# adaLN columns on the tensor engine in float32, four column groups at a time, in a two-layer hybrid diffusion trunk

## The chip, the cores and the metric

One core of a Trainium2 chip runs the whole program in one launch. The metric is the device time of that launch in microseconds (us). The engines are PE (the tensor engine; PEld is its weight load), DVE (vector), ACT (scalar), POOL (GpSimd) and SP, whose queue issues most of the DMAs. Every engine works through its own instructions in order, and waits on semaphores where it needs another's result.

## The reference, cut to what matters

Two layers work on 128 context tokens and 512 latent tokens of 1024 channels. Each layer takes six modulation vectors of 1024 channels (a shift, a scale and a gate for each of its two halves) from a conditioning vector, one set for the context tokens and one for the latent tokens:

```python
mod = silu(c) @ w_mod + b_mod        # c: c_ctx for the context tokens, c for the latent ones
sh1, sc1, g1, sh2, sc2, g2 = jnp.split(mod, 6, axis=-1)
h = rmsnorm(x, p['norm1_g']) * (1.0 + sc1) + sh1
y, s_fin = parallel_mixer(h, s0, p)  # DeltaNet, Hyena, FNet, gated merge
x = x + g1 * y
h = rmsnorm(x, p['norm2_g']) * (1.0 + sc2) + sh2
x = x + g2 * swiglu(h, p['w_gu'], p['w_down'])
```

All arrays are float32. `w_mod` has 2 x 1024 x 6144 elements, so each layer's modulation reads 24 MB for two vectors.

## The kernel before

Channels lie on the 128 partitions and tokens along them: a tensor of 1024 channels is eight tiles of 128 x 640. An "adaLN column" is 128 consecutive outputs of the modulation, so a layer has 48: 0 to 7 are the shift and 8 to 15 the scale of the first norm, 16 to 23 the first gate, 24 to 39 the shift and scale of the second norm, 40 to 47 the second gate. `self.mod[l]` holds them as [128, 2 vectors, 48].

The large products run in three fp32r products each (weights and activations are split into a high and a low part, `wh`/`wl` on the weight side), 320 tokens at a time (`gemm`, `mm3`). ACT writes a unit's high part and POOL its low part. Raw weight tiles `wr` come in two turning buffers through the SP queue (`wload`). The second sub-layer (`ffn`) computes each pair of a gate and an up tile with seven block products instead of eight (`pair`), and the sums that this takes, of weights (`wsum`) and of results (`add` in `pair`), are DVE's.

The order of instructions is fixed when the kernel is built. A main stream issues the large products; side streams (norms, filters, scans, adaLN) are generators whose steps are slipped in by `pump`, after every second contraction tile, as soon as a count of engine time kept by `tick` says that their inputs are there. A step yields a `hint`, a time by which the next one may be issued early. `finish` issues what is left of a stream.

adaLN is computed in two ways. `mods_pe` (line 720) makes columns 0 to 11 of layer 0: the stationary operand is 128 x 2 (the two conditioning vectors), the moving one 128 x 512 of `w_mod` (tiles `A<-in_wm`), in float32, and the rows that result are turned by small products against the identity. `mods` (line 675) makes all other columns on DVE, from a transposed `w_mod` and a copy of both vectors on every partition (`cs`, 1 MB, input `cc`): a column is two 128 x 512 loads into `U` buffers and four multiply-and-sum instructions, whose sums land in `mh`, and one small instruction adds halves and bias into `mod`. Each multiply-and-sum shows as two rows of the trace, `CUSTOM_DVE_ANT_0 A<-U,A` and `DVE_READ_ACCUMULATOR2_ANT mh<-`. `mods` runs five times:

- columns 12 to 27 of layer 0 from the start on, beside the first norm and the input projection (line 2122)
- 28 to 37 of layer 0, or 34 to 39 of layer 1, beside the gates of branch a (line 1887)
- 38 to 47 of layer 0, or 40 to 47 of layer 1, beside the merge of branch b and the output projection (line 1922), finished before the second norm
- 0 to 33 of layer 1 beside layer 0's second sub-layer (line 2139)

The first norm of layer 0 needs columns 0 to 15. `rstd` makes 1 / rms, and `norm` writes `na` (gain times 1 + scale) and then the tiles of h.

Of the kernel before, what the change touches and what calls it, by code (L numbers as in the profile page):

```python
# [18 lines left out]
P = 128  # L19
D = 1024  # L20
# [14 lines left out]
MP = 3  # L35
# [36 lines left out]
def _plan():  # L72
    """the order of use: whole tiles, and pairs of a gate and an up tile for the seven products"""
    p = [("w", k) for k in _stream() if k[0] not in ("g", "u", "d")]
    for kind, g in _ffn_order():
        if kind == "gu":
            for j in GROUPS[g]:
                p += [("s", j)] if j >= WHOLE else [("w", ("g", j)), ("w", ("u", j))]
        else:
            p += [("w", ("d", g, m)) for m in range(0, 8, 2)]  # L80
    return p
# [9 lines left out]
def _parked(key):  # L91
    """whether the split tile stays for one half of the tokens after the other, in a place of its own"""
    k, m = (key[0], key[-1]) if isinstance(key, tuple) else (None, None)
    return (k == "o" and m >= O_SPLIT or k in ("g", "u") and m == 1 or k == "in" and m // P in QKV_ORDER[1:Q_SPLIT]
            or k == "d" and key[1] == len(GROUPS) - 1 and m >= D_SPLIT)
# [10 lines left out]
# ---------------------------------------------------------------- tables that depend on shapes alone  # L106
# [126 lines left out]
# ---------------------------------------------------------------- layout of the inputs  # L233
# [5 lines left out]
def _pack(i):  # L239
# [4 lines left out]
    o["cc"] = np.broadcast_to(np.stack([f["c_ctx"], f["c"][0]])[None], (P, 2, D))  # L244
    o["cT"] = np.stack([f["c_ctx"], f["c"][0]]).reshape(2, KD, P).transpose(2, 1, 0)
    o["wm0"] = f["w_mod"][0][:, :512 * MP].reshape(2, 4, P, MP, 512).transpose(3, 0, 2, 1, 4).reshape(MP, 2, P, 2048)
    o["wmod"] = f["w_mod"].transpose(0, 2, 1).reshape(DEPTH, 48, P, D)
# [53 lines left out]
class _Net:  # L301
# [21 lines left out]
    # ---- allocation  # L323
# [19 lines left out]
    def xps(self):  # L343
        """a bank of either pool"""
        self.nps += 1
        return self.ps() if self.nps % 2 else self.gps()
# [8 lines left out]
    # ---- background work: each step of a side stream is issued once the tensor engine's work issued  # L355
    # so far reaches, by the engines' rates, the time when the step's inputs are there
    def when(self, *aps):
        """the time when what was issued has written these"""
# [8 lines left out]
    def tick(self, eng, op, out, ins):  # L367
# [9 lines left out]
        else:  # L377
            if eng == "pe":
                dt = max(n, 64) * (1 if ins[0].dtype != F32 else 4 if ins[0].shape[0] > 64 else 2) / 2.4e3 + 0.007
# [15 lines left out]
    def on(self, *tiles):  # L395
        """the next step of the stream that runs needs these"""
        self.cur.t = max(self.cur.t, self.when(*[x[:] if not hasattr(x, "ap") else x for x in tiles]))

    def at(self, *tiles):
        """the next step of the stream that runs needs these and nothing of its other steps"""  # L400
# [7 lines left out]
    def ready(self, co):  # L408
        """a stream may yield a test (the time when it is met, or None) or a time its next step may
        be issued early"""  # L410
# [18 lines left out]
    def pump(self):  # L429
        """the streams' ready steps, as long as the main stream keeps its share of the tensor engine"""  # L430
# [19 lines left out]
    def finish_one(self, cos):  # L450
        """the next step of several streams, or of one that they wait for"""
# [6 lines left out]
    def stagger(self, gens, width):  # L458
        """several streams, `width` at a time, each behind the one before it"""
# [32 lines left out]
    # ---- weights  # L492
    def wplan(self, depth):
        """raw tiles in the order of their loads, and units: up to 512 columns that are split at once"""
# [24 lines left out]
    def wload(self, need=-1):  # L519
        """loads of raw tiles up to `need`, and further ones whose room is free by now"""  # L520
# [10 lines left out]
    def wsum(self, r, x):  # L531
        """sums of the four blocks of a gate and an up tile"""
# [12 lines left out]
    def wsplit(self, n):  # L545
        """units up to n, split in two float32r parts"""
# [29 lines left out]
    def wget(self, key):  # L576
        """the units of the next item: all at once, or of a pair one after the other"""
# [13 lines left out]
    def lots(self, n):  # L591
        """places for the next n parked units"""
# [6 lines left out]
    def free(self, seen, drop):  # L599
        """so many more units have come to use, and so many of those in turning buffers had their last"""  # L600
# [32 lines left out]
    def rsqrt(self, r, m):  # L633
        """r = m ** -0.5, Newton's steps from a guess by the bits of m"""
# [9 lines left out]
    # ---- start  # L644
# [30 lines left out]
    def mods(self, l, lo, hi, par=False, ahead=1, hint=0.5):  # L675
        """adaLN columns lo..hi (of 48) of layer l, one per output channel tile"""
# [6 lines left out]
        S = self.A()  # L683
        cs = S[:, 0:2 * D].rearrange("p (s d) -> p s d", s=2)
        ju = S[:, 2 * D:AW]
        nc.sync.dma_start(cs, self.I["cc"])
        q = []

        def load():
            n = at[0]  # L690
            if n < 2 * (hi - lo):
                q.append(self.U())
                nc.sync.dma_start(q[-1], self.I["wmod"][l, lo + n // 2, :, 512 * (n % 2):512 * (n % 2) + 512])
                at[0] += 1

        at = [0]
        for _ in range(ahead):
            load()
        self.on(q[0], cs)
        yield  # L700
        nc.scalar.activation(cs, cs, AF.Silu)
        yield
        for n in range(2 * (hi - lo)):
            j, i = lo + n // 2, n % 2
            if i == 0:
                hv = self.p2.tile([P, 2, 2], F32, tag="mh", name=self.nm("mh"))
            r = q.pop(0)
            if len(q) < (ahead if n < 4 else 1):
                load()
            for s in range(2):  # L710
                nc.vector.tensor_tensor_reduce(out=ju, in0=r, in1=cs[:, s, 512 * i:512 * i + 512], op0=ALU.mult,
                                               op1=ALU.add, scale=1.0, scalar=0.0, accum_out=hv[:, i, s:s + 1])
            if i:
                nc.vector.scalar_tensor_tensor(out=mv[:, :, j], in0=hv[:, 0], scalar=self.par[l][0][:, C_BMOD + j:C_BMOD + j + 1],
                                               in1=hv[:, 1], op0=ALU.add, op1=ALU.add)
            if q:
                self.on(q[0])
            yield hint

    def mods_pe(self):  # L720
        """the first 4 * MP adaLN columns of layer 0, on the tensor engine"""
        nc = self.nc
        mv = self.mod[0] = self.p2.tile([P, 2, 48], F32, tag="mod", name=self.nm("mod"))
        ct = self.p2.tile([P, KD, 2], F32, tag="ct", name=self.nm("ct"), bufs=1)
        nc.sync.dma_start(ct, self.I["cT"])
        nc.scalar.activation(ct, ct, AF.Silu)
        w = {}

        def load(j):
            if j < 2 * MP:  # L730
                w[j] = self.A()
                nc.sync.dma_start(w[j][:, :2048], self.I["wm0"][j // 2, j % 2])

        for j in range(6):
            load(j)
            if j == 3:
                yield
        yield
        pt = self.ps()
        row = {}  # L740

        def turn(j):
            for k in range(4):
                n = 4 * j + k
                nc.tensor.transpose(pt[:, 2 * n:2 * n + 2], row[j][0:2, k * P:k * P + P], self.ident[0:2, 0:2])

        for j in range(MP):
            ps = self.ps()
            for i in range(2):
                self.on(w[2 * j + i])  # L750
                yield
                for k in range(4):
                    nc.tensor.matmul(ps[0:2, :512], ct[:, 4 * i + k], w[2 * j + i][:, k * 512:k * 512 + 512],
                                     start=i == 0 and k == 0, stop=i == 1 and k == 3)
                load(2 * j + i + 6)
                if j and not i:
                    turn(j - 1)
            row[j] = self.Tt()
            nc.scalar.copy(row[j][0:2, :512], ps[0:2])
        yield  # L760
        turn(MP - 1)
        n = 4 * MP
        for s in range(2):
            nc.vector.tensor_tensor(out=mv[:, s, 0:n], in0=pt[:, :2 * n].rearrange("p (j s) -> p s j", s=2)[:, s],
                                    in1=self.par[0][0][:, C_BMOD:C_BMOD + n], op=ALU.add)

    # ---- RMSNorm
    def sq_add(self, k, c=None):
        """running sum of the squares of x's channel tile k, on all tokens or a chunk of them"""
# [11 lines left out]
    def rstd(self, u, n, w):  # L781
        """1 / rms(x) of n * w tokens from u on, on all partitions"""
# [23 lines left out]
    def wait(self, c):  # L806
        """for 1 / rms(x) of a chunk"""
# [3 lines left out]
    def norm(self, l, gcol, sh, scl, new, place):  # L811
        """h = rmsnorm(x) * (1 + sc) + sh, split in two float32r parts"""
# [37 lines left out]
    def need(self, n):  # L850
        """steps of the norm until n channel tiles of chunks of h are issued"""
# [13 lines left out]
    def norm_blocks(self, l, gcol, sh, scl):  # L865
        """h by blocks (half of the channels) x (half of the tokens), and the sums of blocks for the seven
        products"""
# [34 lines left out]
    # ---- x in and out of DRAM  # L902
# [4 lines left out]
    # ---- Hyena's filters  # L907
    def sin_mlp(self, ps, M, scale, bias, out, n):
        """out = sin(scale * ps + bias), the argument brought within half a turn first"""
# [1326 lines left out]
```

## Time and profile before

| | |
|---|---|
| median of 3 runs | 2922.06 us (2921.55 to 2927.12) |
| span of the profiled execution | 2920.5 us |
| PE busy | 2570.7 us, 88% |
| DVE busy | 2191.0 us, 75% |
| POOL busy | 1372.3 us, 47% |
| ACT busy | 1017.4 us, 35% |
| HBM read | 294.89 MB |

PE is the busiest engine, but the share of the span is an average over stages; rows of stretches tell more. A float32 matmul shows as two records (two passes), an fp32r one as one. Every instruction stands under one line, because a helper records it, so rows are told apart by the names of their tiles: `pg` and `ps` are accumulators, `wh` and `wl` the split weights, `mh` and `mod` belong to adaLN.

### The profile page before, as it was taken

How to read it: one execution, taken by the hardware profiler on the slowest of the kernel's cores; microseconds unless marked ns; L12 is line 12 of the kernel's file. 1: busy time of each engine (PE TensorE's matmuls, PEld its weight loads, DVE VectorE, ACT ScalarE, POOL GpSimd, SP SyncE). 2: the span in 40 equal slices, each digit the busy share in tenths (PEclk: the TensorE clock that was granted, in tenths of full speed). 3: DMA queues.
4: the chain of work that ended last, by engine and by line, in shares of the span. 5: the costliest groups of instructions: out<-in, count | busy, mean ns of one | idle time of the engine just before them, and what ended most of it. 6: DMA issues, size and time to landing. Idle time of an engine off the chain costs nothing. (4 is left out here: it accounts for less than half of the span.)

```text
span 2920.5 us, 53508 instructions
## 1 busy us (share of the span) xinstructions
PE 2570.7 (88%) x20996; PEld 2423.8 (83%) x20996; DVE 2191.0 (75%) x4162; ACT 1017.4 (35%) x2148; POOL 1372.3 (47%) x1228
## 2 busy tenths in 40 slices
PE   5897879879998888888898988788899988999998
PEld 1686878879998888878897768788899988999997
DVE  7787996774647899889966679977746468877665
ACT  2454223322332243223334552333323322444342
POOL 2333425442335475555543436353523354777662
PEclk8898989989999899999998999899999998999999
DMA  7442221343554223333322221212335542222222
GB/s 277 143 151 84 71 83 54 103 144 130 201 185 152 86 90 114 105 118 105 109 96 93 94 88 68 83 53 97 134 130 199 187 152 73 66 80 88 79 80 80
DMA packets 112044, 330.35 MB, mean 113 GB/s; under 512 B 12186, under 2 KB 26522, under 8 KB 103776
## 3 DMA queue, kind: packets, MB, share of 16 engines
q1 hardware_dynamic: 110352, 319.06, 31.9%
q0 software_dynamic: 1440, 7.87, 0.8%
q8 instruction: 165, 2.70, 0.4%
q14 instruction: 87, 0.71, 0.1%
HBM read 294.89 MB, written 37.24 MB: 114 GB/s over the span
## 5 line engine op out<-in xcount | busy, mean ns | idle before, releaser
L2185 PE MATMUL pg<-A,wh 128*128 128x320 f32 (+1 forms) x6304 | 1491.7, 324 | 115.3 <-DVE T L2185 46.5
L2185 PEld LDWEIGHTS pg<-A,wh 128*128 128x128 f32 (+1 forms) x6304 | 1096.4, 196 | 168.7 <-issue 56.5
L2185 POOL TENSOR_TENSOR wl<-wr,wh 128x512 fp32r<-128x512 f32 (+2 forms) x486 | 694.5, 1444 | 813.0 <-ACT wh L2185 773.9
L2185 PE MATMUL pg<-A,wl 128*128 128x320 f32 (+1 forms) x3152 | 1005.9, 319 | 1.3 <-POOL wl L2185 1.1
L2185 PEld LDWEIGHTS pg<-A,wl 128*128 128x128 f32 (+1 forms) x3152 | 618.0, 196 | 4.6 <-POOL wl L2185 3.4
L2185 ACT CAST wh<-wr 128x512 fp32r<-128x512 f32 (+2 forms) x486 | 284.4, 611 | 399.6 <-PE pg L2185 287.6
L2185 PE MATMUL ps<-A,wh 128*128 128x320 f32 x1696 | 386.7, 315 | 15.4 <-ACT wh L2185 15.4
L2185 DVE CUSTOM_DVE_ANT_0 A<-U,A 128x512 f32<-128x512 f32 x336 | 324.8, 967 | 14.3 <-DMA U<-in_wmod_dram 7.0
L2185 PEld LDWEIGHTS ps<-A,wh 128*128 128x128 f32 x1696 | 292.1, 193 | 16.9 <-ACT wh L2185 16.7
L2185 PE MATMUL ps<-A,wl 128*128 128x320 f32 x848 | 268.4, 316 | 8.0 <-POOL wl L2185 7.7
L2185 PE MATMUL ps<-A,A 32*32 32x32 f32 (+5 forms) x2984 | 212.1, 248 | 51.1 <-DVE A L2185 49.3
L2185 POOL TENSOR_TENSOR wl<-U,wh 128x512 fp32r<-128x512 f32 x160 | 238.2, 1509 | 30.7 <-ACT wh L2185 30.6
L2185 PEld LDWEIGHTS ps<-A,A 32*32 32x32 f32 (+2 forms) x2984 | 183.7, 150 | 63.1 <-DVE A L2185 50.6
L2185 DVE TENSOR_TENSOR A<-A 128x120 f32<-128x120 f32 (+22 forms) x690 | 209.5, 367 | 11.7 <-DMA A<-hyS 8.8
L2185 POOL TENSOR_TENSOR A<-A,A 128x640 fp32r<-128x640 f32 (+5 forms) x84 | 121.0, 1453 | 161.0 <-ACT A L2185 153.0
L2185 PE MATMUL pg<-A,A 128*128 128x320 f32 x1056 | 168.2, 319 | 10.0 <-ACT A L2185 9.6
L2185 PEld LDWEIGHTS ps<-A,wl 128*128 128x128 f32 x848 | 163.6, 193 | 12.0 <-POOL wl L2185 11.9
L2185 PEld LDWEIGHTS pg<-A,A 128*128 128x128 f32 x1056 | 162.7, 195 | 12.7 <-ACT A L2185 9.8
L2185 DVE TENSOR_TENSOR T<-T,T 128x320 f32<-128x320 f32 (+1 forms) x139 | 120.8, 869 | 68.0 <-ACT T L2185 63.0
L2185 ACT CAST wh<-U 128x512 fp32r<-128x512 f32 x160 | 99.1, 621 | 168.5 <-PE pg L2185 51.3
L2185 DVE STREAM_TRANSPOSE A<-A 32x1024 f32<-32x1024 f32 x72 | 148.8, 2092 | 1.3
L2185 DVE TENSOR_TENSOR U<-ps,U 128x512 f32<-128x512 f32 x144 | 78.0, 543 | 92.0 <-PE ps L2185 64.8
(164 smaller groups left out, 3085.8 us busy)
## 6 DMA issues: line engine op xcount, KB each, us to landing
wr<-in_wbig_dram SPq DMA_DIRECT2D x272, 512.0 KB, 3.7
U<-in_wmod_dram SPq DMA_DIRECT2D x168, 256.0 KB, 4.3
A<-hT SPq DMA_DIRECT2D x32, 1024.0 KB, 8.7
kSp<-U SPq DMA_DIRECT2D x40, 256.0 KB, 2.0
U<-kSp SPq DMA_DIRECT2D x40, 256.0 KB, 5.5
hyS<-T SPq DMA_DIRECT2D x24, 320.5 KB, 3.3
A<-in_wm_dram SPq DMA_DIRECT2D x6, 1024.0 KB, 11.0
A<-in_cc_dram SPq DMA_DIRECT2D x6, 1024.0 KB, 5.3
```

Of the source, the lines that this page charges most:

```text
L2185: return f(*a, **k)
```

## The change

The transposed copy of `w_mod`, the copies of the vectors on all partitions (`cc`) and `mods_pe` go away; all 96 columns take one path. Per column j, one load brings 128 x 1024 of `w_mod` (512 KB, all eight contraction tiles) into half of an `A` buffer. Eight float32 matmuls follow, with 32 stationary columns each (the two conditioning columns and 30 others that come out of use) and 128 moving ones; contraction tiles k and k + 4 accumulate in output partitions 32g to 32g + 31, g = k mod 4, so four matmuls in a row stand in four different column groups of the array. ACT copies the 128 x 128 result to SBUF, and one more float32 matmul with that copy as the stationary operand and a 128 x 2 selection matrix `fold` as the moving one adds the four partial sums and turns the result; DVE adds the bias. The column's last matmul is issued with the step of the next column.

At the start, columns 0 to 15 of layer 0 run with four `A` buffers (eight places) and nothing on DVE but the bias; columns 16 to 27 follow with one buffer (two places). The other three calls keep their columns. In `tick`, the count of time for a matmul with 32 output partitions is halved or quartered, which also concerns the 32 x 32 products of the DeltaNet inverse.

```diff
-    o["cc"] = np.broadcast_to(np.stack([f["c_ctx"], f["c"][0]])[None], (P, 2, D))
...
-    o["wmod"] = f["w_mod"].transpose(0, 2, 1).reshape(DEPTH, 48, P, D)
+    o["wmod"] = f["w_mod"].reshape(DEPTH, KD, P, 48, P).transpose(0, 3, 2, 1, 4).reshape(DEPTH, 48, P, D)
...
-                dt = max(n, 64) * (1 if ins[0].dtype != F32 else 4 if ins[0].shape[0] > 64 else 2) / 2.4e3 + 0.007
+                dt = max(n, 64) * (1 if ins[0].dtype != F32 or out.shape[0] == 32 else 4 if ins[0].shape[0] > 64 else 2) / 2.4e3 + 0.007
...
+    def cond(self):
+        nc = self.nc
+        ct = self.kp.tile([P, 2 * KD + 30], F32, name="ct")
+        nc.vector.memset(ct[:, 2 * KD:], 0.0)
+        nc.sync.dma_start(ct[:, :2 * KD], self.I["cT"])
+        nc.scalar.activation(ct[:, :2 * KD], ct[:, :2 * KD], AF.Silu)
+        self.ct = [ct[:, 2 * k:2 * k + 32] for k in range(KD)]
+        self.fold = self.kp.tile([P, 2], F32, name="fold")
+        nc.vector.tensor_tensor(out=self.fold, in0=self.ident[:, 0:2], in1=self.ident[:, 32:34], op=ALU.add)
+        for g in (64, 96):
+            nc.vector.tensor_tensor(out=self.fold, in0=self.fold, in1=self.ident[:, g:g + 2], op=ALU.add)
+
+    def mods(self, l, lo, hi, par=False, tiles=1, hint=0.5):
...
+        S = [self.A() for _ in range(tiles)]
+        place = [x[:, D * i:D * i + D] for x in S for i in range(2)]
+        w = {}
+        def load(j):
+            if j < hi:
+                w[j] = place[(j - lo) % len(place)]
+                nc.sync.dma_start(w[j], self.I["wmod"][l, j])
+        def turn(j, row):
+            ps = self.ps()
+            nc.tensor.matmul(ps[:, 0:2], row, self.fold, start=True, stop=True)
+            nc.vector.tensor_scalar(out=mv[:, :, j], in0=ps[:, 0:2], scalar1=self.par[l][0][:, C_BMOD + j:C_BMOD + j + 1],
+                                    scalar2=None, op0=ALU.add)
+        for j in range(lo, lo + len(place)):
+            load(j)
+        last = None
+        for j in range(lo, hi):
+            self.on(w[j], *([last[1]] if last else []))
             yield hint
...
+            if last:
+                turn(*last)
             ps = self.ps()
             for i in range(2):
...
+                for g in range(4):
+                    k = 4 * i + g
+                    nc.tensor.matmul(ps[32 * g:32 * g + 32, :P], self.ct[k], w[j][:, k * P:k * P + P],
+                                     start=i == 0, stop=i == 1)
+            row = self.U()[:, :P]
+            nc.scalar.copy(row, ps[:, :P])
+            load(j + len(place))
+            last = j, row
+        self.on(last[1])
+        yield hint
+        turn(*last)
...
-        m = self.bg(self.mods_pe())
         n = self.bg(self.embed())
-        d = self.gm = self.bg(self.mods(0, 4 * MP, 28, ahead=5))
...
+        self.step(n)
+        self.cond()
+        m = self.bg(self.mods(0, 0, MODS0, tiles=4))
+        self.step(m)
+        while not (n.done and m.done):
+            self.finish_one([co for co in (n, m) if not co.done])
+            if m.t > 20.0 and not self.nunit:
+                self.free(0, 0)
+        self.gm = self.bg(self.mods(0, MODS0, MODS1))
```

## Rows read from the trace of the kernel before

**Rows 1.** Groups by line on DVE: count | busy us, mean ns | idle before.
```profile
L2185 DVE CUSTOM_DVE_ANT_0 A<-U,A 128x512 f32<-128x512 f32 x336 | 324.8, 967 | 14.3 <-DMA U<-in_wmod_dram 7.0 <-ACT A L2185 0.9
...
L2185 DVE SCALAR_TENSOR_TENSOR mod<-mh,par 128x2 f32<-128x2 f32 x84 | 43.4, 516 | 3.0
...
L2185 DVE DVE_READ_ACCUMULATOR2_ANT mh<- 128x1 f32 x336 | 26.9, 80 | 0.0
```
**Rows 2.** Stretches, PE rows on tile `wl`: length, PE busy (count), clock, DMA.
```profile
51.10:348.10 297.00, 97.17 (x301) 0.88 0.33 114
1536.30:1813.30 277.00, 97.88 (x301) 0.91 0.24 86
943.10:1462.90 519.80, 261.10 (x801) 0.92 0.32 105
2404.30:2831.30 427.00, 249.12 (x801) 0.98 0.25 81
```
**Rows 3.** The same stretches and others, all engines: PE, PEld, DVE, ACT, POOL, clock.
```profile
348.10:663.90 315.80, 265.92 (x3706) 250.03 (x3705) 250.13 (x530) 103.92 (x243) 138.71 (x159) 0.90 0.29 94
1813.30:2123.00 309.70, 262.34 (x3706) 247.50 (x3705) 246.74 (x504) 103.60 (x243) 140.32 (x159) 0.92 0.27 89
...
943.10:1462.90 519.80, 448.74 (x2758) 435.40 (x2757) 470.20 (x832) 166.54 (x316) 291.60 (x197) 0.92 0.32 105
2404.30:2831.30 427.00, 414.42 (x2758) 410.59 (x2757) 322.20 (x507) 166.68 (x315) 280.01 (x197) 0.98 0.25 81
```
**Rows 4.** The latter two stretches, DVE rows on tile `mh` alone: busy (count).
```profile
943.10:1462.90 519.80, 31.32 (x200) 0.92 0.32 105
2404.30:2831.30 427.00, 5.01 (x20) 0.98 0.25 81
```
**Rows 5.** Timeline from 1340 us: start, length, instruction, count, idle before.
```profile
1342.57 0.46 PE L2185 MATMUL ps<-A,wh 128*128 128x320 f32 x2
...
1344.64 1.75 DVE L2185 CUSTOM_DVE_ANT_0 A<-U,A 128x512 f32<-128x512 f32 x1
...
1346.43 0.69 DVE L2185 CUSTOM_DVE_ANT_0 A<-U,A 128x512 f32<-128x512 f32 x1
...
1348.33 0.87 PE L2185 MATMUL pg<-A,wh 128*128 128x320 f32 x2 [5.15 <-DVE T L2185]
...
1349.26 0.74 PE L2185 MATMUL pg<-A,wh 128*128 128x320 f32 x2
```
**Rows 6.** Stretch of the merge of branch b, columns as in rows 3.
```profile
895.00:940.00 45.00, 33.08 (x188) 31.04 (x187) 37.56 (x67) 12.91 (x19) 24.13 (x16) 0.89 0.41 147
```
**Rows 7.** Timelines at 978 and 624 us: PE waits behind multiply-and-sums.
```profile
978.54 1.23 PE L2185 MATMUL ps<-small,T 128*80 128x1 f32 x8 [6.75 <-DVE T L2185]
...
624.29 4.71 PE L2185 MATMUL ps<-small,U 128*128 128x128 f32 x20 [10.37 <-DVE U L2185]
```
**Rows 8.** Timeline of the start: when tiles land, columns end, products begin.
```profile
12.65 0.22 ACT L2185 ACTIVATE ct<-ct 128x16 f32<-128x16 f32 x1 [10.63 <-DMA ct<-in_cT_dram]
...
42.14 0.41 PE L2185 MATMUL ps<-small,T 2*128 2x2 f32 x4
...
47.33 0.08 DVE L2185 DVE_READ_ACCUMULATOR2_ANT mh<- 128x1 f32 x1
...
47.72 0.24 DVE L2185 TENSOR_TENSOR mod<-ps,par 128x12 f32<-128x12 f32 x2
47.91 0.24 DVE L2185 SCALAR_TENSOR_TENSOR na<-mod,par 128x8 f32<-128x8 f32 x2
...
50.05 1.00 PE L2185 MATMUL pg<-A,wh 128*32 128x320 f32 x2 [7.50 <-ACT A L2185]
```
**Rows 9.** DMA in the first 60 us: GB/s in 40 slices of 1.5 us.
```profile
GB/s 0 205 341 278 375 410 423 416 415 437 415 431 421 415 415 407 399 410 445 437 425 392 404 332 119 29 279 403 403 395 314 277 415 27 0 0 0 11 0 0
```
**Rows 10.** Timeline: float32 passes of 512 moving columns with 2 stationary ones, one group.
```profile
30.05 7.03 PE L2185 MATMUL ps<-A,ct 128*2 128x512 f32 x16
```
**Rows 11.** Timeline: float32 passes of 64 x 64 in four tiles, between 320-column products.
```profile
281.98 0.46 PE L2185 MATMUL pg<-A,wh 128*128 128x320 f32 x2
282.27 0.31 PE L2185 MATMUL pg<-A,wl 128*128 128x320 f32 x1
282.51 0.34 PE L2185 MATMUL ps<-A 64*64 64x64 f32 x8
...
283.38 0.30 PE L2185 MATMUL ps<-A,A 64*64 64x64 f32 x8
283.60 0.56 PE L2185 MATMUL pg<-A,wh 128*128 128x320 f32 x2
```
**Rows 12.** Timeline: float32 passes with one moving column.
```profile
1524.04 0.71 PE L2185 MATMUL ps<-small,T 128*80 128x1 f32 x8
```
**Rows 13.** Groups by line on ACT: a copy of the size that the change adds.
```profile
L2185 ACT COPY A<-ps 128x128 f32<-128x128 f32 x24 | 5.5, 265 | 3.2 <-PE ps L2185 3.0
```
**Rows 14.** Page, DMA issues: KB each, us to landing.
```profile
wr<-in_wbig_dram SPq DMA_DIRECT2D x272, 512.0 KB, 3.7
U<-in_wmod_dram SPq DMA_DIRECT2D x168, 256.0 KB, 4.3
```
**Rows 15.** Timeline: SP issues of adaLN loads early in layer 0's second sub-layer.
```profile
1037.21 11.17 SPq L2185 DMA_DIRECT2D U<-in_wmod_dram  x2
```

More of the change, by code (lines that the diff above doesn't have):

```diff
@@ L34 @@
 EPS = 1e-6
-MP = 3
+MODS0, MODS1 = 16, 28
 MAGIC = float(0x5F3759DF)
@@ L243, in _pack @@
     o["xT"] = x.T.reshape(KD, P, T).transpose(1, 0, 2)
-    o["cc"] = np.broadcast_to(np.stack([f["c_ctx"], f["c"][0]])[None], (P, 2, D))
-    o["cT"] = np.stack([f["c_ctx"], f["c"][0]]).reshape(2, KD, P).transpose(2, 1, 0)
-    o["wm0"] = f["w_mod"][0][:, :512 * MP].reshape(2, 4, P, MP, 512).transpose(3, 0, 2, 1, 4).reshape(MP, 2, P, 2048)
-    o["wmod"] = f["w_mod"].transpose(0, 2, 1).reshape(DEPTH, 48, P, D)
+    o["cT"] = np.stack([f["c_ctx"], f["c"][0]]).reshape(2, KD, P).transpose(2, 1, 0).reshape(P, 2 * KD)
+    o["wmod"] = f["w_mod"].reshape(DEPTH, KD, P, 48, P).transpose(0, 3, 2, 1, 4).reshape(DEPTH, 48, P, D)
     keys = _stream()
@@ L673, in load_par @@
         self.par[l] = (t, ab)
-    def mods(self, l, lo, hi, par=False, ahead=1, hint=0.5):
+    def cond(self):
[10 more added lines that the diff above has]
+    def mods(self, l, lo, hi, par=False, tiles=1, hint=0.5):
         nc = self.nc
@@ L682, in mods @@
         mv = self.mod[l]
[L683 to L726, printed above, removed]
+        S = [self.A() for _ in range(tiles)]
+        place = [x[:, D * i:D * i + D] for x in S for i in range(2)]
         w = {}
         def load(j):
[L730 to L734, printed above, removed]
-            load(j)
[L736 to L747, printed above, removed]
+            if j < hi:
+                w[j] = place[(j - lo) % len(place)]
+                nc.sync.dma_start(w[j], self.I["wmod"][l, j])
@@ L748, in mods_pe @@
             ps = self.ps()
             for i in range(2):
[L750 to L765, printed above, removed]
+                for g in range(4):
+                    k = 4 * i + g
+                    nc.tensor.matmul(ps[32 * g:32 * g + 32, :P], self.ct[k], w[j][:, k * P:k * P + P],
+                                     start=i == 0, stop=i == 1)
@@ L768, in sq_add @@
+            row = self.U()[:, :P]
[3 more added lines that the diff above has]
+        self.on(last[1])
+        yield hint
+        turn(*last)
     def sq_add(self, k, c=None):
@@ L1886, in mixer @@
         self.mg = [v4(self.A()) for _ in range(2)]
-        gm = [self.bg(self.when_met(self.dpr, self.mods(l, (28, 34)[l], (38, 40)[l])))]
+        gm = [self.bg(self.when_met(self.dpr, self.mods(l, (MODS1, 34)[l], (38, 40)[l])))]
         self.gates(l, "a", self.mg)
@@ L2119, in run @@
         self.x = self.x_tile()
-        m = self.bg(self.mods_pe())
         n = self.bg(self.embed())
-        d = self.gm = self.bg(self.mods(0, 4 * MP, 28, ahead=5))
-        for co in (n, m, d, m, *(n,) * (KD + 1), m, m, n, d, m, m, n):
-            self.step(co)
-        self.free(0, 0)
-        for co in (d, d, d, d, m, d, d, m, d, d, m):
-            self.step(co)
+        self.step(n)
[7 more added lines that the diff above has]
+        self.gm = self.bg(self.mods(0, MODS0, MODS1))
         self.ff = self.bg(self.filters(0))
         self.step(self.ff)
-        self.finish(m, n)
         self.rs, self.hn = [n, n], 0
```

## The prediction

> **What bounds the kernel now.** I read the DVE groups first, since they are what the change removes. adaLN costs DVE 324.8 + 26.9 + 43.4 = 395 us for 84 columns, 4.7 us a column, a multiply-and-sum taking 967 ns on average [rows 1]. DVE is not the busiest engine, PE is, so this is worth only what PE waits for. The kernel itself offers the measure: its two layers issue the same products, and in layer 1 one long stretch has almost no adaLN in it. I cut both layers at the same products (the count of `wl` products in a stretch is the same, 801 and 801) and compared lengths. From the end of the merge to the last group of the second sub-layer, layer 0 takes 519.8 us and layer 1 427.0 [rows 2]. PE's instruction counts are equal (2758), DVE is 470.2 us busy against 322.2, and PE's granted clock is 0.92 against 0.98 [rows 3]. Rows on `mh` come five to a column: 40 columns fall into the stretch of layer 0, 4 into that of layer 1 [rows 4]. So 36 columns on DVE cost 92.8 us of path here, 2.6 us each.
>
> The timeline tells how. PE runs dry at about 1343 us, and while it waits 5.15 us for a sum that DVE owes it, DVE works on two multiply-and-sums of the next layer's adaLN, one of them 1.75 us long. Afterwards a pair of products takes 0.74 us instead of 0.46: the wait also cost the clock [rows 5]. In the projection stretch layer 0, with 12 columns, is 20 us longer than layer 1, which has none there (297.0 against 277.0) [rows 2]. So DVE's lateness bounds the second sub-layer of layer 0 and shares in the bound elsewhere; the sub-layer of layer 1 is bound by PE (414.4 of 427 us busy [rows 3]).
>
> **What a column costs PE afterwards.** A float32 pass of 512 columns in one column group takes (7.03 - 0.6)/15 = 0.43 us [rows 10], taking 0.6 us as the drain of the last, so one of 128 columns takes 0.107 us, and eight matmuls of two passes each would take 16 x 0.107 = 1.72 us one behind the other. No row has four column groups of 128 rows. The nearest is the DeltaNet's 64 x 64 passes in four tiles: 64 of them, 64 columns each and so 0.054 us alone, fill 283.60 - 282.27 - 0.15 = 1.18 us between two ordinary products, where one behind the other would be 3.4 us. A quarter of that is 0.86, so four run at once, with 0.32 us for entering, leaving and 16 rounds of weights; entering is visible, 282.51 - 282.27 = 0.24 us against 0.15 [rows 11]. Two tiles in that pattern share their rows and differ in their columns, as the new ones do. I take 1.72/4 = 0.43, plus 0.2 of the 0.32, since there are four rounds and not sixteen. The sum over groups has a 128-column weight load and two passes; with 80 columns a pass takes under 0.09 us [rows 12], so I take 0.22 for two. A column then costs 0.85 us of PE; the bounds are 0 (it falls into time in which PE waits anyway) and 2.15 (no overlap: 1.72 + 0.2 + 0.22).
>
> The Trainium skill, "TensorE: Matmul & The Clock Gate", section "Measured speedup vs the span model", has three column groups at 2.38 times the speed of one, not three times. The rows above show four tiles at four times, less the entering. By the page's share, 0.79, the eight matmuls would take 0.54 us and not 0.43, an estimate that adds 0.11 x 84 = 9 us to the forecast.
>
> The rest is hidden. ACT gets 96 copies of 0.265 us [rows 13], 25 us in all on an engine that is 35% busy; an uncovered copy delays only its own column, whose last matmul is issued a step later. DVE keeps one small instruction a column. SP loses six 1 MB loads; its column loads now wait for PE to have read a place, and the next `wr` tile is queued behind them. Before, such loads held SP for 11.17 us, waiting on DVE [rows 15], so I put nothing down for that.
>
> **The sum, by stretch.**
>
> - Start, to the first product at 50.05 us. Before, PE had turned its twelve columns at 42.6, but DVE worked on four more until 47.4, then wrote `mod` and `na` [rows 8]. After, sixteen columns (8.4 MB) come behind the x tiles, and what is queued ahead of them has landed by 12.65 [rows 8]; at about 415 GB/s [rows 9] that is 20 us, 33 in all, 34.5 with a weight tile between. The last column's products, copy, sum and bias take 2 us more, and `na` to the first product 2.1 [rows 8]: 39 us, so -11. Bounds 0 and -14.
> - Projection: 297.0 becomes 277.0 plus 12 x 0.85 = 287, so -10 (bounds +10 and -20).
> - Gates of branch a: the stretches hardly differ (315.8 with ten columns, 309.7 with six [rows 3]). One wait of 10.37 us behind DVE [rows 7] held four columns; I give back 7 of it, and add 16 x 0.85 = 13.5: +6.5. Bounds -15 and +13.5.
> - Merge of branch b: in 45 us PE idles 45 - 33.08 = 11.9 us and loses 0.11 x 45 = 5 us to the clock while DVE is 83% busy [rows 6]; layer 1 repeats it. I give back two thirds, 11 us in each layer, because ACT and POOL are in these waits too, less four columns each: -22 + 7 = -15. Bounds -30 and 0.
> - Second sub-layer of layer 0 with the output projection: -92.8 + 36 x 0.85 = -62. Next late there is PE itself, as in layer 1. The wait of 6.75 us ahead of the second norm [rows 7] ends behind multiply-and-sums that layer 1 has too (four columns); for both layers I give back 5 each and add 8 x 0.85: -3. Together -65, bounds -98 and -40.
> - A new wait. PE is in order: a column whose weights or whose copy is late stops the products behind it. A tile of 512 KB lands 3.7 us after its issue [rows 14], and with two places a pair of columns can't come faster than 3.7 + 0.85 us against 1.7 us of work: up to 1.4 us a column, for the 46 columns outside start and sub-layer 0 to 64 us. Products of the main stream stand between the steps, so I take 10.
>
> Sum: -11 - 10 + 6.5 - 15 - 65 + 10 = -84.5. The profiled span of 2920.5 us becomes 2836; the median of the runs is 1.6 us above it, so 2837 us.
>
> The changed time for 32-partition products in `tick` also shifts the order of the scans. No row prices that; the same gates stretch in two orders gives 315.8 and 309.7 [rows 3], so I allow 6 us either way.
>
> **The rivals.**
>
> *No overlap of the column groups* (the change doesn't do what it says). Each column costs 2.15 us: 1.3 x 84 = +109, and at the start sixteen columns take PE 34 us from 13 us on, so its 11 us go too: 2957 us, slower. It decides at 1.85 us a column, where the whole gain of 84 us is spent. Against it stand the four tiles at once [rows 11]; for it, that no row has 128 rows in four groups.
>
> *Columns that come late.* If nearly every column outside the start waits its 1.4 us, 80 x 1.4 = 112 us replace the 10: 2939 us, slower, and from 1 us a column on there is no gain. For it: two places and a landing time of 3.7 us. Against it: a column is wanted only every few us.
>
> *Only the second sub-layer and the start gain.* Elsewhere DVE's waits are replaced by those on ACT and POOL: 2920.5 - 11 - 62 + 46 x 0.85 = 2887, with the median 2888.
>
> *The columns outside the sub-layer fall into PE's idle time* and cost nothing, and the new wait doesn't come: 2837 - 10 - 39 = 2788.
>
> **How the numbers follow.** The forecast, 2837, has 55% (about 2810 to 2865); gain in the sub-layer and start alone 20%; columns for nothing 12%; late columns 7%; no overlap 6%. The range reaches from 2785, the fourth rival, to 2905, the third with some of the new wait in it; it leaves out the slower ones and tails, some 15 to 20%. A change of 0.2% (6 us) is about what a measurement of this kernel can tell from none. Faster by more: 0.88; within: 0.03; slower: 0.09.
>
> **What would show it.** In the changed profile: 16 passes of a column within 0.5 to 0.6 us, against 1.7 under the first rival; layer 0's long stretch at about 458 us with PE's clock near 0.98, and waits for DVE `T` gone from it; first product at about 39 us; PE busy up by about 84 x 0.85 - some overlap; no long waits of PE on `A<-in_wmod` or on an ACT copy. The forecast is wrong if those waits exceed 1 us a column, if the passes don't overlap, or if the stretch stays above 490 us, which would mean that DVE's sums were not late because of adaLN.

## The result, and the profile after

The changed kernel takes 2853.02 us (median of four runs, 2847.94 to 2854.90) against 2921.81 before: a ratio of 0.9753, 95% interval [0.9733, 0.9773], or 69 us less. The forecast was 2837 us, 84.5 less: the sign and the range held, and the gain came 16 us short; the mechanism held where most of the gain was forecast and failed at the start. The profiled execution spans 2846.2 us, 74.3 less than before, because it was the quickest of the four; stretches below are of that one.

Busy times on the page of the kernel after:

```profile
span 2846.2 us, 56258 instructions
PE 2595.5 (91%) x22664; PEld 2455.5 (86%) x22664; DVE 1870.7 (66%) x3504; ACT 1030.8 (36%) x2235; POOL 1331.2 (47%) x1228
```

DVE lost 320 us and PE gained 25. The groups by line that are new, of PE, ACT and DVE (count | busy us, mean ns | idle before):

```profile
L2151 PE MATMUL ps<-A,ct 128*32 128x128 f32 x1536 | 69.5, 304 | 24.2 <-ACT T L2151 14.0 <-DMA A<-in_wmod_dram 10.1
L2151 PE MATMUL ps<-fold,U 128*128 128x2 f32 x192 | 33.1, 242 | 15.3 <-ACT U L2151 15.1
L2151 ACT COPY U<-ps 128x128 f32<-128x128 f32 x96 | 25.4, 264 | 103.4 <-PE ps L2151 102.7
L2151 DVE TENSOR_SCALAR mod<-ps,par 128x2 f32<-128x2 f32 x96 | 20.5, 216 | 62.1 <-PE ps L2151 61.8
```

These stand where the 395 us of [rows 1] stood. Next, the same stretches as in [rows 2, 3], and the one that ends with the merge of branch b, cut at the same products (start:end, length, then busy time and count of PE, PEld, DVE, ACT and POOL, granted clock, DMA share, GB/s). The first row is the merge's stretch before, for comparison with the fourth; the others are after:

```profile
663.90:943.10 279.20, 260.33 (x1814) 254.18 (x1813) 158.96 (x304) 83.82 (x179) 107.58 (x83) 0.97 0.48 170
61.50:363.80 302.30, 256.74 (x1896) 220.13 (x1896) 200.11 (x415) 126.09 (x292) 114.75 (x136) 0.91 0.30 101
363.80:671.10 307.30, 269.24 (x3887) 255.09 (x3886) 213.24 (x428) 103.81 (x251) 132.64 (x159) 0.92 0.29 93
671.10:951.20 280.10, 266.61 (x1994) 258.70 (x1994) 146.48 (x278) 84.61 (x187) 106.23 (x83) 0.98 0.51 176
951.20:1399.20 448.00, 441.07 (x3370) 430.58 (x3369) 306.24 (x505) 175.44 (x350) 271.99 (x197) 0.99 0.36 113
2339.30:2757.00 417.70, 410.39 (x2759) 406.40 (x2757) 306.32 (x471) 168.34 (x316) 274.86 (x197) 0.99 0.25 78
```

Layer 0's second sub-layer went from 519.8 to 448.0 us: PE is busy for 441 of them, at a clock of 0.99 and not 0.92. Its longest waits over the whole stretch (total us, times, longest), the three of before (line 2185) and the two of after (line 2151):

```profile
PE pg L2185 <- DVE T L2185: 35.6, 15, 5.2
PE ps L2185 <- ACT wh L2185: 15.4, 5, 4.0
PE ps L2185 <- DVE T L2185: 6.7, 1, 6.7
PE ps L2151 <- DVE T L2151: 3.2, 1, 3.2
PE ps L2151 <- POOL wl L2151: 2.1, 1, 2.1
```

Against that, the projection's row begins 10 us later than in [rows 2] and is 5 longer. The timeline of the start shows why it begins later (start, length, instruction, idle before; rows of PEld, and some of DVE, ACT and SP, are left out):

```profile
21.88 1.08 PE L2151 MATMUL ps<-A,ct 128*32 128x128 f32 x16
23.03 0.27 ACT L2151 COPY U<-ps 128x128 f32<-128x128 f32 x1 [1.08 <-PE ps L2151]
23.34 0.59 PE L2151 MATMUL ps<-fold,U 128*128 128x2 f32 x2 [0.39 <-ACT U L2151]
23.40 0.90 SPq L2151 DMA_DIRECT2D wr<-in_wbig_dram  x2
23.86 1.08 PE L2151 MATMUL ps<-A,ct 128*32 128x128 f32 x16
30.55 0.41 ACT L2151 CAST wh<-wr 128x256 fp32r<-128x256 f32 x1 [7.26 <-DMA wr<-in_wbig_dram]
...
33.49 0.24 ACT L2151 COPY U<-ps 128x128 f32<-128x128 f32 x1
33.62 0.83 DVE L2151 TENSOR_TENSOR T<-T,T 128x640 f32<-128x640 f32 x1 [10.08 <-ACT T L2151]
33.79 0.59 PE L2151 MATMUL ps<-fold,U 128*128 128x2 f32 x2 [8.85 <-ACT U L2151]
...
60.28 1.00 PE L2151 MATMUL pg<-A,wh 128*32 128x320 f32 x2 [2.43 <-ACT A L2151]
```

A column takes 1.98 us here (21.88 to 23.86), in three parts: passes, a wait for the copy, the sum. The weight tile `wr` was issued at 23.40, its cast on ACT waited for it until 30.55, and everything behind that cast waited too: the column's copy, a square for the first norm, with it DVE, and PE for 8.85 us.

A column in the sub-layer, where PE runs at full speed:

```profile
1085.26 0.31 PE L2151 MATMUL pg<-A,wl 128*128 128x320 f32 x1
1085.41 0.28 PE L2151 MATMUL ps<-fold,U 128*128 128x2 f32 x2
1085.61 0.64 PE L2151 MATMUL ps<-A,ct 128*32 128x128 f32 x16
1086.19 0.56 PE L2151 MATMUL ps<-A,wh 128*128 128x320 f32 x2
```

From the sum at 1085.41 to the next product at 1086.19 it is 0.78 us (0.20 and 0.58), where 0.85 was forecast.

### The profile page after: what moved, and what is told of

It reads as the page before. It is cut to its first block, busy times and chain, and to the rows that moved or that the text cites. A ratio compares the mean times of both kernels' runs of the same rounds, so it can differ in the third digit from the quotient of the medians.

```text
span 2846.2 us, 56258 instructions
## 1 busy us (share of the span) xinstructions
PE 2595.5 (91%) x22664; PEld 2455.5 (86%) x22664; DVE 1870.7 (66%) x3504; ACT 1030.8 (36%) x2235; POOL 1331.2 (47%) x1228
## 5 line engine op out<-in xcount | busy, mean ns | idle before, releaser
L2151 PE MATMUL pg<-A,wh 128*128 128x320 f32 (+1 forms) x6304 | 1477.1, 321 | 53.7 <-DVE T L2151 14.8
L2151 PEld LDWEIGHTS pg<-A,wh 128*128 128x128 f32 (+1 forms) x6304 | 1081.6, 194 | 107.5 <-issue 22.3
L2151 POOL TENSOR_TENSOR wl<-wr,wh 128x512 fp32r<-128x512 f32 (+2 forms) x486 | 677.5, 1407 | 777.5 <-ACT wh L2151 745.4
L2151 PEld LDWEIGHTS pg<-A,wl 128*128 128x128 f32 (+1 forms) x3152 | 610.7, 194 | 3.6 <-POOL wl L2151 2.6
L2151 PE MATMUL ps<-A,wh 128*128 128x320 f32 x1696 | 379.6, 310 | 0.0
L2151 PEld LDWEIGHTS ps<-A,wh 128*128 128x128 f32 x1696 | 283.4, 188 | 3.4 <-issue 2.4
L2151 POOL TENSOR_TENSOR wl<-U,wh 128x512 fp32r<-128x512 f32 x160 | 225.9, 1425 | 52.9 <-ACT wh L2151 52.9
L2151 DVE TENSOR_TENSOR T<-T,T 128x320 f32<-128x320 f32 (+1 forms) x139 | 133.4, 960 | 100.6 <-ACT T L2151 96.4
L2151 POOL TENSOR_TENSOR A<-U,A 128x320 fp32r<-128x320 f32 (+1 forms) x48 | 53.8, 1127 | 165.1 <-ACT A L2151 165.1
```

What stands on the lines that cost most here:

```text
L2151: return f(*a, **k)
```

## The experiments

Ratios are to the kernel before, on the same chip. "After" is the changed kernel, and all edits are to it unless said otherwise.

**What the columns cost, on DVE and on PE.** Two kernels leave columns out, one from each side.

```diff
--- before, in mods, per half column
-            for s in range(2):
-                nc.vector.tensor_tensor_reduce(out=ju, in0=r, in1=cs[:, s, ...], ..., accum_out=hv[:, i, s:s + 1])
```

> The kernel before with the 336 multiply-and-sums on DVE left out (adaLN columns past the first twelve are then wrong); their loads, the small add of each column and all else stay. It gives the whole price of adaLN on DVE. Theory A: 93 us in the stretch of the second sub-layer and 20 in the projection, 15 to 25 in the two merges and the waits ahead of the second norm, so 2922 becomes 2785 to 2800; the projection stretch of layer 0 is then near 277 us. Rival (only the sub-layer was bound by DVE): 2825, projection near 297.

Measured: 2761.4 us, 0.9431 [0.9403, 0.9460]. The multiply-and-sums cost 160 us of path by the spans (2920.5 - 2760.2) and 164 by the medians on that chip, more than the 122 to 137 that I had read out of the trace. They are 352 of the 395 us that adaLN keeps DVE busy; the small instructions stay in.

```diff
--- after, in mods, per column
+            if not (l == 0 and lo == 0):
+                nc.vector.tensor_scalar(out=mv[:, :, j], in0=self.ct[0][:, 0:2], ...)
+                load(j + len(place))
+                continue
...
```

> The changed kernel with the matmuls, the copies and the sums of the 80 columns past the start left out (their values are then wrong); the loads and the small bias instruction stay. It gives the price of the columns on PE. Theory A: 0.78 us a column and nearly all on the path, so 2853 - 80 x 0.78 = 2790, a few us lower where PE waited for a load. Rival (half of it fell into PE's waits): 2820.

Measured: 2781.4 us, 0.9498 [0.9472, 0.9523]. Eighty columns on PE cost 72 us by the medians and 66 by the spans (2846.2 - 2780.1), 0.8 to 0.9 each: about their own work on PE, 0.78. So the change trades a price of 160 for one of about 70. The 19 us from there to the measured 69 are mostly the sixteen columns of the start, which `e6_no_columns` keeps: its first `wl` product starts at 59.8 us, that of `e5_no_sums` at 45.0. The sub-layer of layer 0 in the two, `e5_no_sums` first:

```profile
896.30:1318.90 422.60, 412.21 (x2758) 406.53 (x2757) 314.98 (x511) 167.86 (x316) 274.31 (x197) 0.99 0.39 128
911.10:1341.20 430.10, 414.62 (x2758) 408.06 (x2757) 317.63 (x505) 167.39 (x316) 276.56 (x197) 0.99 0.35 117
```

By stretch, in us of path (before less `e5_no_sums`, after less `e6_no_columns`):

| stretch (by the count of `wl` products) | DVE's price | PE's price | before to after | forecast |
|---|---|---|---|---|
| up to the first product | 5.9 | 1.3 | +10.2 | -11 |
| projection, layer 0 | 13.8 | 14.8 | +5.4 | -10 |
| gates of branch a, layer 0 / 1 | 17.7 / -0.6 | 15.7 / -1.8 | -8.6 / -1.3 | +6.5 in all |
| merge of branch b, layer 0 / 1 | 9.5 / 9.7 | 7.9 / 7.9 | +0.9 / -0.7 | -15 in all |
| second sub-layer and output projection, layer 0 / 1 | 97.1 / 8.1 | 18.0 / -0.5 | -71.6 / -9.4 | -65 in all |

(The stretches that the table leaves out are 0.8 us in "before to after", and 2.7 in PE's price, 2.5 of them in the projection of layer 1, which has no column. PE's price in the row of the start is of columns 16 and up alone.)

DVE's price less PE's doesn't give a row's change exactly. If the change did nothing else, the kernels without the sums and without the columns would take equally long outside the start, but `e6_no_columns` is 4.3 us longer than `e5_no_sums` in the projection, 6.7 shorter in the gates of layer 0, 3.6 longer in the two merges and 7.5 longer in the sub-layer of layer 0. No run tells why, so a single price is good to some 7 us.

**Do four column groups run at once?** The first rival, built: all eight products of a column into the same 32 partitions, one behind the other.

```diff
-                    nc.tensor.matmul(ps[32 * g:32 * g + 32, :P], self.ct[k], w[j][:, k * P:k * P + P],
-                                     start=i == 0, stop=i == 1)
-            row = self.U()[:, :P]
+                    nc.tensor.matmul(ps[0:32, :P], self.ct[k], w[j][:, k * P:k * P + P],
+                                     start=k == 0, stop=k == KD - 1)
+            row = self.U()[:32, :P]
```

> The changed kernel with all eight matmuls of a column in one column group (32 output partitions, all eight contraction tiles accumulate there), the sum over 32 rows. Nothing is left out. In the changed kernel 16 passes of a column take 0.37 us from first to last start, 0.78 us in all with the sum. Theory A (four groups run at once): the passes take 16 x 0.107 = 1.7 us here, about 1.25 us more a column, 80 columns x 1.25 = 100 us more outside the start and 13 more in it; what falls into PE's waits is saved, so 2853 becomes 2930 to 2965, slower than the kernel before. Rival (groups don't matter, small matmuls are cheap anyway): 2853.

Measured: 2942.2 us, 1.0048 [1.0025, 1.0070], half a percent slower than before. Its column in the timeline:

```profile
1100.19 0.38 PE L2151 MATMUL ps<-small,U 32*128 32x2 f32 x2
1100.51 1.93 PE L2151 MATMUL ps<-A,ct 128*32 128x128 f32 x16
1102.37 0.56 PE L2151 MATMUL pg<-A,wh 128*128 128x320 f32 x2
```

Sixteen passes in a row take 1.93 us, and in four groups 0.64: (1.93 - 0.64)/12 = 0.108 us for each of the twelve passes that no longer stand in line, the 0.107 that I had from [rows 10]. So four run at once, and the gain hangs on it: layer 0's sub-layer is 49 us longer than after (497.1), 1.44 a column for 34 columns. Rival one, at 2957 us, would have been near had the groups not overlapped.

From its first pass to the next product a column's matmuls take 1.86 us in one group and 0.58 in four, 3.2 times less, or 0.80 of four. The Trainium skill, "TensorE: Matmul & The Clock Gate", section "Measured speedup vs the span model", gives 2.38 for three groups, 0.79 of three. The trace has the same share, though for four groups and 128 moving columns, where the page's row has 512. Here the shortfall is the entering and leaving, since rounds of four passes start 0.109 us apart, as single passes do in one group, and my sum already held 0.2 us for it. The page's 9 us would have been counted twice.

**The start.** First, the weight tiles' loads ahead of the columns':

```diff
+        self.wload()
         m = self.bg(self.mods(0, 0, MODS0, tiles=4))
```

> The changed kernel with one edit: the first two raw weight tiles are loaded ahead of the adaLN tiles, not after the sixth column. In the changed kernel PE stands still from 24.9 to 33.8 us at the start, because ACT's copy of a column's result is queued behind a weight cast whose tile landed only at 30.5. Theory A (ACT's queue holds the copies): the hole of 8.9 us goes, the first product moves from 60.3 to about 52 us, 2853 becomes about 2845. Rival B (the column loads themselves are late, because each waits for PE to have read its place): the hole only moves, first product near 60 us, 2853.

Measured: 2841.4 us, 0.9709 [0.9684, 0.9735]; the first `wl` product starts at 52.7 us, not 61.1. The casts now run without a wait, and the 8.85 us hole is gone:

```profile
22.56 1.44 ACT L2152 CAST wh<-wr 128x256 fp32r<-128x256 f32 x3
```

Second, a column's sum issued behind the next column's passes:

```diff
-            self.on(w[j], *([last[1]] if last else []))
+            self.on(w[j])
             yield hint
-            if last:
-                turn(*last)
...
             load(j + len(place))
+            if last:
+                turn(*last)
```

> The changed kernel with one edit: the matmul that sums a column over its four groups is issued behind the eight matmuls of the next column, not ahead of them. In the changed kernel the columns of the start come every 1.98 us: eight matmuls 0.87 at half clock, then ACT's copy, then the sum 0.52, and only then the next column. Theory A: the wait for the copy is covered, a column comes every 1.4 to 1.5 us, sixteen columns save 8 us; the hole behind the weight cast stays or shrinks; 2853 becomes about 2845. Rival B (loads bound the columns): no gain at the start. Elsewhere at most 2 us, since PE waited for copies little there.

Measured: 2844.7 us, 0.9716 [0.9690, 0.9742]; first `wl` product at 54.9. The hole stays, but a column comes every 1.52 us:

```profile
33.76 0.59 PE L2151 MATMUL ps<-fold,U 128*128 128x2 f32 x2 [10.00 <-ACT U L2151]
```

Both together:

> Both edits: weight tiles loaded first, and the sum of a column issued behind the next one's matmuls. Theory A: the two add up, first product at 42 to 45 us, 16 us less than the changed kernel, 2837: what the forecast had for the start comes back. Rival B: under 5 us.

Measured: 2838.0 us, 0.9693 [0.9667, 0.9720]; first `wl` product at 46.4. The two gains nearly add (8.3 + 6.1 of the 14.7 us at the first product), and no other stretch moves by more than 3 us, though the span gains only 10.0, since the gates, the merge and the sub-layer of layer 0 together give back 6.9. So these two orders of issue are 14.7 us of the start's miss of 21. To see whether the hole was the copy's place on ACT's queue, the copies of the start alone were given to DVE:

```diff
-            nc.scalar.copy(row, ps[:, :P])
+            if l == 0 and lo == 0:
+                nc.vector.tensor_copy(out=row, in_=ps[:, :P])
+            else:
+                nc.scalar.copy(row, ps[:, :P])
```

> The changed kernel with one edit: at the start alone the copies of the columns' sums from PSUM are made by DVE and not by ACT. The theory (an ACT copy queued behind a weight cast that waits for its DMA stops PE for 8.85 us, and each column pays for a copy that nothing hides): the long hole goes, since DVE has nothing in front of these copies that waits for a weight tile; the short wait for the copy stays, since the sum is still issued ahead of the next column. First wl product about 52 us instead of 61, the time about 2844 us (ratio to the kernel before about 0.973). The rival (the hole only hides that the column loads themselves come late): PE waits for the column tiles instead, first product at 59 or later, time within 3 us of the changed kernel's 2853.

Measured: 2849.6 us, 0.9751 [0.9727, 0.9774]; first `wl` product at 61.8. Neither explanation held, though the rival's numbers came out: the hole is as long as before, and PE waits in it for a copy and not for a column's tile.

```profile
30.13 0.40 ACT L2154 CAST wh<-wr 128x256 fp32r<-128x256 f32 x1 [10.81 <-DMA wr<-in_wbig_dram]
...
32.42 1.36 ACT L2154 ACTIVATE T<-A 128x640 f32<-128x640 f32 x2
33.19 0.84 DVE L2154 TENSOR_TENSOR T<-T,T 128x640 f32<-128x640 f32 x1 [8.61 <-ACT T L2154]
33.95 0.21 DVE L2154 TENSOR_SCALAR mod<-ps,par 128x2 f32<-128x2 f32 x1
34.08 0.28 DVE L2154 COPY U<-ps 128x128 f32<-128x128 f32 x1
34.41 0.59 PE L2154 MATMUL ps<-fold,U 128*128 128x2 f32 x2 [8.78 <-DVE U L2154]
```

DVE, in order as well, stands in front of an add of squares for the first norm, whose square is on ACT behind the cast that waits for `wr`. So the theory needs one more link: the cast that waits for its DMA holds not its own queue alone, but each in-order engine that takes something from that queue. Moving the load cured it, moving the copy did not.

**The order of the side streams.** The changed time for 32-partition products in `tick`, undone:

```diff
-                dt = max(n, 64) * (1 if ins[0].dtype != F32 or out.shape[0] == 32 else 4 if ...
+                dt = max(n, 64) * (1 if ins[0].dtype != F32 else 4 if ...
```

> The changed kernel with the planner's old count of time for products with 32 output partitions. The column's matmuls are then counted at four times the new time and the scans' 32 x 32 products at twice, so side streams come in another order; the work is the same. Theory A: order alone is worth little, 2853 within 8 us. Rival: part of the 8.6 us that the first DeltaNet stretch of layer 0 gained comes from this count; then 2860 or more, and that stretch is back near 315 us.

Measured: 2852.1 us, 0.9736 [0.9704, 0.9768], no difference to after. Single stretches move (merge of layer 0 +6.7 us, gates of layer 1 +5.2, the projection -5.2), the median doesn't; I had allowed 6 us either way. The gates of layer 0 stay at 307.3 us, so their gain doesn't come from this count.

**Places for the columns.** After, PE waits in the merge of branch b for column tiles, which it never did before (waits in 895 to 947 us):

```profile
PE ps L2151 <- DMA A<-in_wmod_dram: 2.9, 5, 0.8
```

Four places instead of two for that call, on top of `e3_both`:

```diff
-        self.gm = self.bg(self.mods(l, (38, 40)[l], 48))
+        self.gm = self.bg(self.mods(l, (38, 40)[l], 48, tiles=2))
```

> The kernel with both edits of the start, and four places instead of two for the columns beside the merge of branch b. In the changed kernel PE waits there 3 us in each layer for a column's tile. Theory A (two places are too few, the load's landing time shows): the waits on the column tiles go, 5 to 6 us less than with the two edits alone. Rival: the waits are replaced by those on ACT and POOL, no difference.

Measured: 2826.8 us, 0.9658 [0.9635, 0.9681], 11 us below `e3_both`, whose interval this one just overlaps; the spans differ by 11.4. The two merges are 3.2 and 3.6 us shorter, and PE's waits on column tiles there fall from 3.9 and 2.6 us to 0.8 and 0.9; of the rest, 3.7 stand in the gates of layer 0, which the edit doesn't touch, and that part stays unexplained. The same for the twelve columns of the projection (`self.mods(0, MODS0, MODS1, tiles=2)`):

> The version with weights first, the sum a column later and four places in branch b's merge, and now four places for the twelve columns of the projection too. If the 1.23 us a column that the projection paid were mostly waits on column tiles (3.8 us in all), the first 300 products get 3 to 4 us shorter and the time is about 2823 us. The rival: those waits are replaced by waits on x and weight tiles, or the second tile of places keeps another tile from its load: no difference to the 2827 us of the version without it, or up to 4 us longer.

Measured: 2815.3 us, 0.9625 [0.9602, 0.9649], the lowest of the kernels that make all columns. The projection is 2.7 us shorter, about as expected, but not for the reason expected: PE still waits 3.24 us for a column's tile there, against 3.3 in two waits without the edit. The longer of those two, and the one that is left:

```profile
105.08 1.08 PE L2152 MATMUL ps<-A,ct 128*32 128x128 f32 x16 [2.62 <-DMA A<-in_wmod_dram]
107.31 0.65 PE L2152 MATMUL ps<-A,ct 128*32 128x128 f32 x16 [3.24 <-DMA A<-in_wmod_dram]
```

The gates of layer 0 gave another 5.7 us, again outside the edit, so what gained here stays open. The median is 11.5 us below the version without it, the profiled span 5.1, and the two intervals overlap: that it is faster is likely, by how much is open.

## Why the prediction was right, point by point

**The bound was read rightly.** DVE's sums were late because adaLN stood between them: PE's 42 us of waits for DVE `T` in the sub-layer became 3.2, and its clock went from 0.92 to 0.99. The comparison of the two layers [rows 2] gave 92.8 us for 36 columns; with the sums left out the stretch became 422.6, so the 40 columns cost 97. The comparison was a little low because layer 1's own four columns, which it set to nothing, cost 8.1 us; 3.6 us went the other way, since without the sums layer 0's stretch is still that much longer (422.6 against 419.0). PE's busy time rose by 25 us and not by about 71, as the list of signs had it: the new products are busy 102.6 us (69.5 + 33.1), the old ones on PE were 24.1, so PE's other work takes some 50 us less. Most of that goes with the clock: in the sub-layer the same 2758 records are busy 448.7 us before, at 0.92, and 412.2 in `e5_no_sums`, at 0.99.

**Sub-layer: forecast -65, measured -81.** The mechanism held, three sizes were off to the same side. A column's work on PE was 0.78 and not 0.85; 34 columns fell into the stretch and not 40; and the 18 us that they cost are 0.53 each, less than their work, so part of them lay in time in which PE waits anyhow (PE's idle time in the stretch is 15.5 us without the columns, 430.1 - 414.6, and 6.9 with them). In layer 1, where I gave back 5 less the work of four columns, no column is left in the stretch, and it became 9.4 us shorter.

**Start: forecast -11, measured +10.** This is the step that failed: "an uncovered copy delays only its own column". The prediction's own bullet on the new wait says the opposite, that a late copy stops the products behind it, but it puts a price on late tiles alone. PE is in order, and the sum, which needs the copy, is issued ahead of the next column's passes; so each copy delays all later columns (0.46 us each: 1.98 against 1.52), and the one copy that stood behind a waiting cast stopped them all for 8.85 us. The estimate of 34.5 us for the last column took DMA's pace (1.25 us a column) as the only bound and PE's work at full speed, 0.85; at the speed of the start a column takes 1.52 even with the sum late. With both orders mended the first product comes at 45.6 us, against 39 forecast and 50.05 before. Between 16.0 and 43.1 us PE then has one wait, of 0.64 us, so the 6.6 us that are left of the miss are mostly PE's own work, at half speed until 38.3 us (last section). The rival that I should have priced is the copy's wait.

**Projection: forecast -10, measured +5.** Both terms were mis-sized. The difference of 20 us between the layers isn't all adaLN's (13.8 without the sums), and a column cost 14.8/12 = 1.23 us of path, not 0.85, with 3.8 us of waits on column tiles in it. The two measured prices would make this row +1, not +5; the other 4 us are of the differences that no run explains.

**Gates: forecast +6.5, measured -9.9.** DVE's price in layer 0 is 17.7 us, of which I gave back 7, having counted the one long wait [rows 7] alone; PE's, 15.7 for ten columns there, was put at 13.5 for sixteen. In layer 1 neither shows. The two prices alone make -2 in layer 0, so most of its -8.6 stays unexplained, and that this stretch gained that much is luck as far as the forecast goes.

**Merges: forecast -15, measured 0.** DVE's price, 9.6 each, was near the 11 that I took. PE's, 7.9 each, was put at four columns; now all ten, or eight, fall into this stretch, at 0.8 to 1 us, some of it the waits on column tiles. The gain is taken back by the columns, not by ACT or POOL, as the third rival had it.

**New wait: forecast 10, measured 27.** On the page PE waits 10.1 us for column tiles and 16.9 for copies:

```profile
PE ps L2151 <- ACT U L2151: 16.9, 19, 8.8
PE ps L2151 <- DMA A<-in_wmod_dram: 10.1, 13, 2.2
```

The tiles are as forecast, 0.13 us for each of the 80 columns past the start, far from the 1.4 of the second rival. The copies were named in the forecast and not priced; 14.2 us of their waits fall into the start. Measured, all of this lies inside the stretches above and is no term beside them.

The errors of single terms, from -16 to +21, partly cancel. Sub-layer and gates gave 32 us more than forecast, start, projection and merges 52 less. That the time came within 16 us of the forecast owes as much to this as to the sum. The range, made from the rivals, was wide enough for it; of the single bounds, those of the start, 0 and -14, were broken. The chances don't fit each other: the two rivals that end slower have 13% together, and slower was given 9%.

## What to carry to other kernels

A step moved from a late engine to a busy one is worth the path price of the first less that of the second: leave each out in a kernel of its own and subtract, for a busy time (352 us of sums on DVE here) says neither (160, and about 70). On an in-order engine, issue what needs another engine's answer behind the next independent work, and issue a load ahead of the first instruction that waits for it by more than its landing time (7 us at this start, from 23.40 to 30.55), because a waiting cast stops also the engines that take from its queue. Two layers cut at the same instruction counts give a good first price, low by what the lighter layer pays itself.

## What the runs showed of the hardware that I hadn't expected

Four groups of 32 float32 columns run at the full four times: passes start 0.109 us apart in one group, and rounds of four follow at the same distance. What is lost, 0.58 us against 1.86/4 = 0.47, is lost at the edges.

The slow speed of the start doesn't show in the granted clock. That reads 1.00 from 14 to 44 us in `e3_both`, but the trace holds no record of the clock before 38.6 us, and the view counts such time as full speed. The same sixteen passes take 1.08 us before 39 us and 0.64 after, and their rounds of four start 0.214 us apart until 38.3 us and 0.109 from 39.0 on, the ratio of the engine's two levels, 1.2 and 2.4 GHz:

```profile
14.00:44.00 30.00, 26.30 (x302) 18.76 (x302) 16.15 (x45) 9.31 (x26) 4.69 (x15) 1.00 0.95 365
```

```profile
36.16 1.08 PE L2152 MATMUL ps<-A,ct 128*32 128x128 f32 x16
37.17 0.59 PE L2152 MATMUL ps<-fold,U 128*128 128x2 f32 x2
37.69 1.07 PE L2152 MATMUL ps<-A,ct 128*32 128x128 f32 x16
38.69 0.39 PE L2152 MATMUL ps<-fold,U 128*128 128x2 f32 x2
39.00 0.64 PE L2152 MATMUL ps<-A,ct 128*32 128x128 f32 x16
```

Before the change of speed PE had worked since 16 us with one wait, of 0.64 us. After the change as made, with a wait at each column, the first record of the clock stands at 76.0 us, and so does the change of speed: products of 320 columns start 0.27 us apart at 74.5 us and 0.15 at 77. So the 0.91 of the stretch from 61.5 us counts 14.5 us of half speed as full. In the kernel before, the first record is at 21.2 us, and the passes of 512 columns start 0.85 us apart until 21.1 us and 0.43 after. At a start, then, the lengths of instructions tell the speed, and not that column.
